# Moving the later modulation sums of a transformer layer from the matmul engine to GpSimd

## The chip, the cores and the metric

The kernel runs on one core of one Trainium2 chip. Five engines of the core work side by side, each on its own instructions in order: TensorE (PE in the profile; PEld is its weight load), VectorE (DVE), ScalarE (ACT), GpSimd (POOL) and SyncE (SP), which here only issues transfers. An engine that waits holds up everything behind it on that engine. The metric is the device time of one execution in microseconds, as a median over runs.

## The reference

One layer of a diffusion backbone on 512 latent tokens of width 1024 with 256 context tokens. All numbers are float32. What matters here is where the conditioning vector `c` enters:

```python
def adaln(cond, w_mod, b_mod):                  # cond (1, 1024), w_mod (1024, 6144)
    return jnp.split(jax.nn.silu(cond) @ w_mod + b_mod, 6, axis=-1)

sh1, sc1, g1, sh2, sc2, g2 = adaln(c, w_mod[l], b_mod[l])
hx = modulate(rmsnorm(x, norm_attn_g[l]), sh1, sc1)     # the context likewise, with c_ctx
...                                                      # projections, two kinds of attention
x = x + g1 * mixed
hx2 = modulate(rmsnorm(x, norm_ffn_g[l]), sh2, sc2)
x = x + g2 * hierarchical_moe(hx2, ...)                  # 16 experts, each token in two of them
return rmsnorm(x, final_norm_g)
```

`silu(c) @ w_mod` is a vector by a 1024 x 6144 matrix, so each weight is used once. The first 2048 columns (sh1, sc1) are needed at once; the other 4096 (g1, sh2, sc2, g2: "the later columns", 16 MB) only when the attention is done.

## The kernel before

The stages follow each other: normalise the tokens and form the first modulation (to about 60 us), project (to 120), neighbourhood attention with its projections (to 242), latent attention (to 370), output projection and routing (to 427), then the experts, whose weights stream from memory until the end. Outside of the hand-ordered parts (`manual_schedule`) a scheduler orders each engine's instructions when the kernel is built; the order is then fixed. Matmuls of float32 precision are made of three products of high and low parts (`mm3`, lines 57 to 59).

In the neighbourhood attention 32 blocks (four head pairs `p`, two heads `u`, four query tiles `i`; `b` counts them) run one after the other. A block's `na_scores` (L606, L607) go to PSUM; VectorE adds a bias and takes the row maximum (L617, L470); ScalarE takes the exponential; the next block's turn transposes it (`na_turn`, L634). Between them PE gets parts of the next pair's projections (`works`, by the table `NS`). `na_values` (L643) closes a pair.

Every second block also calls `mod_rest(n)`: two loads of 512 KB of the later columns' weights into the ring `raw` (three buffers, queue of SyncE), and four matmuls (L521) whose stationary operand is `sstat`, silu(c) in one column of 32 zeros; the four write to the four quarters of the partitions of one PSUM bank. After eight calls the sums with the bias row (`br`) go to DRAM (`mod_d`), twice in all. Later stages read `mod_d` back: g1 for the latent attention's output weights (L894), then sh2, sc2 and g2.

At the very start GpSimd issues five small loads, first `mp1` (biases and gain of the first modulation), and VectorE adds 1 to a part of it (L142) ahead of all of its normalisation work. GpSimd also fills four `ql` tiles with zeros (L532).

Of the kernel before, what the change touches and what calls it, by code (L numbers as in the profile page):

```python
# [17 lines left out]
P = 128  # L18
# [17 lines left out]
K_TRI, K_IOTA, K_TJ, K_VAL, K_ROW, K_END = 0, 128, 256, 272, 280, 281  # L36


def hybrid_kernel(tc, nc, x_k, x_q, ctx, cvec, w_mod_a, w_mod_b, b_mod_c, b_mod_r, g_ffn_row,
                  w_v, w_kv, w_ql, w_qk, g_q, g_kv, w_uq, w_ukv, rel, w_out_a, w_out_b, w_r, b_r,  # L40
                  w_gate, w_up, w_down, g_fin_row, cpk0, cpk, out):
    sy, ac, ve, pe, gp = nc.sync, nc.scalar, nc.vector, nc.tensor, nc.gpsimd
# [81 lines left out]
    mp1 = cst.tile([P, 4, 12], F32, name="mp1")  # L124
# [4 lines left out]
    ab = cst.tile([P, 4, 8], F32, name="ab")  # L129
    sm = cst.tile([P, 24], F32, name="sm")  # L130
    eps = cst.tile([P, 1], F32, name="eps")
    ve.memset(eps, EPS)
    lg = cst.tile([P, 4, 20], F32, name="lg")
# [365 lines left out]


    ya_d = tc.dram_tile([T, D], F32, name="ya_d")
    zero = nw.tile([P, 512], F32, name="zero")
    ve.memset(zero, 0.0)


    mod_d = tc.dram_tile([2, 4, 512], F32, name="mod_d")
    modf = mod_d.rearrange("r a b -> r (a b)")
    mod_ps = []

    def mod_rest(n):  # L510
        r, k = divmod(n, KT)
        if k == 0:
            br = nw.tile([P, 512], F32, name="br", tag="br", bufs=1)
            ve.memset(br, 0.0)
            rows = br.rearrange("(a b) n -> a b n", b=32)[:, 0, :]
            sy.dma_start(rows, b_mod_r[r])
            mod_ps[:] = bank(7), br, rows
        ps, br, rows = mod_ps
        ws = [load(w_mod_b[r, k, :, q * 1024:(q + 1) * 1024]) for q in range(2)]
# [200 lines left out]
    for b, (p, u, i) in enumerate(blocks):  # L720
        w = b % 8
        if w == 0 and p < 3:
            na_open(p + 1)
        s = na_scores(p, u, i)
        nm = na_max(p, u, i, s)
        if p < 3:
            if w in (3, 5, 7):
                for u_ in range(2):
                    na_part(p + 1, w // 2 - 1, u_, 1)
            if w == 2:  # L730
                na_weights(p + 1, 1, 1)
            if w == 4 and p < 2:
                na_weights(p + 2, 0, 1)
            if w == 6:
                for u_ in range(2):
                    na_bias(p + 1, u_)
        if NS[p][w] > 1:
            pull(1)
        if len(turns) >= (2 if b > 24 else 1):
            na_turn(*turns.pop(0))  # L740
        turns.append((p, u, i))
        na_exp(p, u, i, s, nm)
        if w == 0 and p:
# [541 lines left out]
    with tc.manual_schedule(engines={pe.engine, ve.engine}):  # L1285
# [55 lines left out]
        count = cst.tile([P, NE + 1 + NB * NE], I32, name="count")  # L1341
# [503 lines left out]
def _layout(**n):  # L1845
# [16 lines left out]
    a["w_mod_b"] = c(wm[:, 2048:].reshape(KT, P, 2, 2048).transpose(2, 0, 1, 3))  # L1862
# [4 lines left out]
    a["b_mod_r"] = c(bm[2048:].reshape(2, 4, 512))  # L1867
# [51 lines left out]
```

## Time and profile before

| | |
|---|---|
| median of three runs | 735.29 us (733.8 to 735.91) |
| profiled execution | 733.54 us; span 731.8 us, so 1.7 us lie around the span |
| mean granted clock of TensorE | 0.983 |
| busy: PE, DVE, ACT, POOL | 698.1, 546.4, 447.7, 83.7 us (95%, 75%, 61%, 11% of the span) |
| moved by DMA | 174.58 MB, 239 GB/s over the span |

The profile is one execution. Busy shares are means over all stages; what an edit of one stage is worth is read in that stage's rows.

### The profile page before, as it was taken

How to read it: one execution, taken by the hardware profiler on the slowest of the kernel's cores; microseconds unless marked ns; L12 is line 12 of the kernel's file. 1: busy time of each engine (PE TensorE's matmuls, PEld its weight loads, DVE VectorE, ACT ScalarE, POOL GpSimd, SP SyncE). 2: the span in 40 equal slices, each digit the busy share in tenths (PEclk: the TensorE clock that was granted, in tenths of full speed). 3: DMA queues.
4: the chain of work that ended last, by engine and by line, in shares of the span. 5: the costliest groups of instructions: out<-in, count | busy, mean ns of one | idle time of the engine just before them, and what ended most of it. 6: DMA issues, size and time to landing. Idle time of an engine off the chain costs nothing. (4 is left out here: it accounts for less than half of the span.)

```text
span 731.8 us, 10466 instructions
## 1 busy us (share of the span) xinstructions
PE 698.1 (95%) x3918; PEld 516.9 (71%) x3919; DVE 546.4 (75%) x749; ACT 447.7 (61%) x698; POOL 83.7 (11%) x56
## 2 busy tenths in 40 slices
PE   4999999999999999999999679999999999999995
PEld 3678997767765887868658557777777777777773
DVE  4572457766676795656536778999999999999996
ACT  6451355654555455646644377777777777777763
POOL 1010000000000000000010122222222222221310
PEclk9999999999999999999999769999999999999998
DMA  8931238555476821121179979999999999999673
GB/s 319 409 124 60 73 95 279 194 172 190 144 236 202 288 88 43 60 76 54 59 252 364 346 244 364 362 372 370 353 360 357 358 352 350 358 354 379 239 132 116
DMA packets 39336, 174.58 MB, mean 239 GB/s; under 512 B 5711, under 2 KB 7191, under 8 KB 26992
## 3 DMA queue, kind: packets, MB, share of 16 engines
q1 hardware_dynamic: 34880, 163.72, 61.4%
q0 software_dynamic: 4112, 10.06, 6.3%
q8 instruction: 32, 0.52, 0.3%
q14 instruction: 24, 0.20, 0.1%
q10 hardware_dynamic: 288, 0.08, 0.0%
HBM read 163.00 MB, written 14.79 MB: 243 GB/s over the span
## 5 line engine op out<-in xcount | busy, mean ns | idle before, releaser
L1376 DVE TENSOR_TENSOR el<-ew,eh 128x2048 fp32r<-128x2048 f32 (+1 forms) x106 | 220.6, 2087 | 17.3 <-ACT eh L1373 13.7
L1373 ACT CAST eh<-ew 128x1024 fp32r<-128x1024 f32 x190 | 190.1, 1050 | 43.9 <-PE s L59 29.4
L57 PE MATMUL s<-eh,xh 128*96 128x512 f32 x260 | 104.7, 403 | 1.1 <-ACT xh L62 1.1
L59 PE MATMUL s<-eh,xl 128*96 128x512 f32 x260 | 103.3, 397 | 0.0
L58 PE MATMUL s<-el,xh 128*96 128x512 f32 x260 | 102.8, 395 | 0.0
L1588 POOL DMA_INDIRECT ya_d<-yo,idx x14 | 45.5, 3251 | 140.7 <-DVE yo L1592 140.7
L59 PEld LDWEIGHTS s<-eh,xl 128*96 128x96 f32 x260 | 42.3, 163 | 19.3 <-DVE xl L63 0.7
L57 PEld LDWEIGHTS s<-eh,xh 128*96 128x96 f32 x260 | 42.4, 163 | 18.3 <-ACT xh L62 1.4
L58 PEld LDWEIGHTS s<-el,xh 128*96 128x96 f32 x260 | 42.5, 164 | 17.5 <-DVE el L1376 0.2
L57 PE MATMUL y<-eh,ghh 128*96 128x512 f32 x120 | 48.2, 401 | 0.0
L59 PE MATMUL y<-eh,ghl 128*96 128x512 f32 x120 | 47.3, 394 | 0.0
L58 PE MATMUL y<-el,ghh 128*96 128x512 f32 x120 | 47.2, 393 | 0.0
L470 DVE TENSOR_REDUCE nm<-s 128x1 f32<-128x768 f32 x32 | 30.5, 954 | 19.1 <-PE s L59 18.9
L57 PE MATMUL ps<-wh,hh 128*128 128x512 f32 (+2 forms) x128 | 43.9, 345 | 0.5 <-ACT hh L275 0.3
L59 PE MATMUL ps<-wh,hl 128*128 128x512 f32 (+2 forms) x128 | 43.5, 345 | 0.2 <-DVE hl L277 0.2
L58 PE MATMUL ps<-wl,hh 128*128 128x512 f32 (+2 forms) x128 | 43.4, 341 | 0.0
L1303 POOL MEMSET xg<- 128x1024 f32 x2 | 1.9, 954 | 322.1 <-DMA g<-mod_d 322.1
L57 PE MATMUL ps<-hh,wh 128*128 128x512 f32 (+1 forms) x96 | 36.4, 379 | 0.0
L946 ACT ACTIVATE pr<-s,nm 128x768 f32<-128x768 f32 x32 | 29.1, 908 | 9.8 <-DVE nm L470 9.6
L59 PE MATMUL ps<-hh,wl 128*128 128x512 f32 (+1 forms) x96 | 34.4, 359 | 0.0
L58 PE MATMUL ps<-hl,wh 128*128 128x512 f32 (+1 forms) x96 | 34.2, 357 | 0.0
L1261 POOL DMA_INDIRECT xg<-hx_d,idx x16 | 24.2, 1510 | 65.9 <-PE t L1519 46.7
(360 smaller groups left out, 1455.8 us busy)
## 6 DMA issues: line engine op xcount, KB each, us to landing
ew<-w_gate SPq DMA_DIRECT2D x32, 1024.0 KB, 8.6
ew<-w_up SPq DMA_DIRECT2D x32, 1024.0 KB, 8.0
ew<-w_down SPq DMA_DIRECT2D x32, 1024.0 KB, 9.4
raw<-w_mod_b SPq DMA_DIRECT2D x32, 512.0 KB, 3.8
wm<-w_mod_a SPq DMA_DIRECT2D x16, 512.0 KB, 10.8
raw<-w_qk SPq DMA_DIRECT2D x8, 512.0 KB, 3.4
raw<-w_v SPq DMA_DIRECT2D x4, 512.0 KB, 10.5
ya_d<-zero SPq DMA_DIRECT2D x8, 256.0 KB, 3.2
```

The source lines that it names most:

```text
L57: pe.matmul(ps, lh, rh, start=start, stop=False)
L58: pe.matmul(ps, lh, rl, start=False, stop=False)
L59: pe.matmul(ps, ll, rh, start=False, stop=stop)
L470: ve.tensor_reduce(out=nm, in_=s, axis=AX.X, op=OP.max, negate=True)
L946: ac.activation(pr, s, AF.Exp, bias=nm, accum_out=mla_ssum[h // 2][:, t, h % 2:h % 2 + 1])
L1261: ins = gp.indirect_dma_start(out=xg[e % NX][slice(0, CAP), :], out_offset=None, in_=hx_d, in_offset=bass.IndirectOffsetOnAxis(ap=idx[slic ...
L1303: gp.memset(x_, 0.0)
L1373: ac.copy(wh[:, cs], r[:, cs])
L1376: ve.tensor_tensor(wl[:, cs], r[:, cs], f(wh[:, cs]), op=OP.subtract)
L1588: gp.indirect_dma_start(out=ya_d, out_offset=bass.IndirectOffsetOnAxis(ap=idx[rows, 1, e:e + 1], axis=0), in_=yo[rows, :], in_offset=None, ...
```

## The change

Of the later 4096 columns, cut into eight rows of 512, six rows are summed on GpSimd. Such a row's weights come in two pieces of 1 MB (128 partitions x 4 x 512; `mod_load`, twelve pieces in all, from GpSimd's own queue, into the two halves of the pool `omp`). `mod_weigh` multiplies a piece by silu(c), which stands in `sstat` for each partition, and folds its four parts by additions; the two pieces of a row are added up in `macc`. What is left is a sum over the 128 partitions: `mod_sum` does it with four small matmuls against a column of ones (L544), adds the bias on VectorE and stores the row. The last two rows stay on the matmul engine (`mod_rest`), now all in the last pair's eight blocks, with 256 instead of 512 columns a matmul. The tiles `ab`, `mp1`, `lg` and `count` move to other pools, `zero` is halved, and with `mp1` its load moves behind the four other loads of GpSimd.

```diff
-    gp.dma_start(mp1, b_mod_c)
-    ve.tensor_scalar(mp1[:, :, 4:8], mp1[:, :, 4:8], 1.0, None, op0=OP.add)
     gp.dma_start(gq, g_q)
     gp.dma_start(gkv, g_kv)
     gp.dma_start(wr, w_r)
...
+    gp.dma_start(mp1, b_mod_c)
+    ve.tensor_scalar(mp1[:, :, 4:8], mp1[:, :, 4:8], 1.0, None, op0=OP.add)
...
+    def mod_load(n):
+        w = mod_w[n] = omp.tile([P, 4, T], F32, name=f"wb{n % 2}", tag=f"{n % 2}", bufs=1)
+        gp.dma_start(w, w_mod_b[n // 2, n % 2])
+    def mod_weigh(n):
+        r, h = divmod(n, 2)
+        w = mod_w.pop(n)
+        gp.tensor_tensor(w, w, sstat[:, 4 * h:4 * h + 4, 0:1].to_broadcast([P, 4, T]), op=OP.mult)
+        gp.tensor_tensor(w[:, 0:2, :], w[:, 0:2, :], w[:, 2:4, :], op=OP.add)
+        if h == 0:
+            acc = mod_acc[r] = nw.tile([P, 512], F32, name="macc", tag="macc", bufs=2)
+            gp.tensor_tensor(acc, w[:, 0, :], w[:, 1, :], op=OP.add)
+        else:
+            gp.tensor_tensor(w[:, 0, :], w[:, 0, :], w[:, 1, :], op=OP.add)
+            gp.tensor_tensor(mod_acc[r], mod_acc[r], w[:, 0, :], op=OP.add)
+    def mod_rows(n):
+        br = nw.tile([P, n * P], F32, name="br", tag="br", bufs=1)
+        ve.memset(br, 0.0)
+        return br, br.rearrange("(a b) n -> a b n", b=32)[:, 0, :]
+    def mod_sum(r):
+        acc = mod_acc.pop(r)
+        br, rows_ = mod_rows(1)
+        sy.dma_start(rows_, b_mod_r[r])
+        ps = bank(7)
+        for g in range(4):
+            pe.matmul(ps[g * 32:(g + 1) * 32, 0:P], ones, acc[:, g * P:(g + 1) * P], start=True, stop=True,
+                      tile_position=(0, g * 32))
+        ve.tensor_tensor(br, br, ps[:, 0:P], op=OP.add)
+        sy.dma_start(mod_d[r], rows_)
...
+        w = load(w_mod_c[k])
         for g in range(4):
-            pe.matmul(ps[g * 32:(g + 1) * 32, :], sstat[:, k, :],
-                      ws[g // 2][:, g % 2 * 512:g % 2 * 512 + 512], start=(k == 0), stop=(k == KT - 1),
-                      tile_position=(0, g * 32))
+            pe.matmul(ps[g * 32:(g + 1) * 32, 0:256], sstat[:, k, :], w[:, g * 256:g * 256 + 256], start=(k == 0),
+                      stop=(k == KT - 1), tile_position=(0, g * 32))
...
-        if i % 2:
-            mod_rest(p * 4 + u * 2 + i // 2)
+        if b % 2 == 0 and b // 2 < NP:
+            if b // 2 + 2 < NP:
+                mod_weigh(b // 2)
+                mod_load(b // 2 + 2)
+            else:
+                mod_weigh(b // 2)
+        if b % 4 == 3 and b // 4 > 1:
+            mod_sum(b // 4 - 2)
+        if p == 3:
+            mod_rest(w)
```

What the scheduler made of it is seen at three places. First GpSimd, which in the kernel before does nothing between the `ql` memsets and the latent attention's end. In the changed kernel this is what it issues for one pair of pieces (`wb_1291` and `wb_1344`), up to the first multiply of the next pair (`wb_1409` and `wb_1479`); the names in brackets are the semaphores waited for (DMASW: a load of GpSimd's queue; Pool: an instruction of GpSimd itself):

```order
L523 TENSOR_TENSOR wb_1291<-wb_1291,sstat 128x2048 [waits DMASW7_49]
L524 TENSOR_TENSOR wb_1291<-wb_1291 128x1024 [waits Pool_49]
L523 TENSOR_TENSOR wb_1344<-wb_1344,sstat 128x2048 [waits DMASW0_49]
L527 TENSOR_TENSOR macc<-wb_1291 128x512 [waits Pool_49]
L524 TENSOR_TENSOR wb_1344<-wb_1344 128x1024 [waits Pool_49]
L517 DMA wb_1409<-w_mod_b 128x2048 [waits DMASW1_49,Pool_49]
L529 TENSOR_TENSOR wb_1344<-wb_1344 128x512 [waits Pool_49]
L530 TENSOR_TENSOR macc<-macc,wb_1344 128x512 [waits Pool_49]
L517 DMA wb_1479<-w_mod_b 128x2048 [waits DMASW2_49,Pool_49]
L523 TENSOR_TENSOR wb_1409<-wb_1409,sstat 128x2048 [waits DMASW1_49]
```

The load of the next pair's first piece is issued behind five of the pair's seven instructions, and the multiply that needs it stands four places behind it.

Second PE, at the end of the neighbourhood attention: the last values (`pt`,`nav`), the last transposes (`rsb`) and the first products of the latent attention (`o`). Before:

```order
L643 MATMUL ps<-pt,nav 64x512
L521 MATMUL ps<-raw,sstat 32x512 x2
L643 MATMUL ps<-pt,nav 64x512
L643 MATMUL ps<-pt,nav 64x128 x16
L643 MATMUL ps<-pt,nav 64x512 x2
L486 MATMUL ps<-c_58,rsb 128x128 x4
L57 MATMUL o<-kvh,wkh 128x512
```

and in the changed kernel:

```order
L560 MATMUL ps<-raw,sstat 32x256 x4
L672 MATMUL ps<-c_58,pr 128x128 x4
L57 MATMUL ps<-wh,kvh 128x512
L544 MATMUL ps<-macc,one 32x128 x4
L58 MATMUL ps<-wl,kvh 128x512
L59 MATMUL ps<-wh,kvo 128x512
L681 MATMUL ps<-pt,nav 64x512 x2
L681 MATMUL ps<-pt,nav 64x128 x16
L681 MATMUL ps<-pt,nav 64x512 x2
L485 MATMUL ps<-c_58,rsb 128x128 x4
L544 MATMUL ps<-macc,one 32x128 x4
L57 MATMUL o<-kvh,wkh 128x512
```

The last two of GpSimd's six rows (L544) are summed here, the sixth directly ahead of the latent attention; the other four stand at blocks 11, 15, 19 and 23.

Third VectorE at the same place (`qnl` and `onl` are the last low parts of this stage, `kl` the first of the next). Before:

```order
L525 TENSOR_TENSOR br<-br,ps 128x512 [waits PE_49]
L63 TENSOR_TENSOR qnl<-raw,qnh 128x512 [waits DMAHW2_49,Activation_49]
L63 TENSOR_TENSOR qnl<-raw,qnh 128x512 [waits DMAHW3_49,Activation_49]
L489 TENSOR_TENSOR rsb<-ps,rsb 128x512 [waits Activation_49]
L491 TENSOR_TENSOR onl<-rsb,onh 128x512 [waits Activation_49]
```

and in the changed kernel (DMAHW: a transfer of SyncE's queue):

```order
L563 TENSOR_TENSOR br<-br,ps 128x256 [waits PE_49]
L82 COPY pt<-ps 128x512 [waits PE_49]
L63 TENSOR_TENSOR qnl<-raw,qnh 128x512 [waits DMAHW0_49,Activation_49]
L63 TENSOR_TENSOR qnl<-raw,qnh 128x512 [waits DMAHW1_49,Activation_49]
L534 MEMSET br 128x128 [waits DMAHW3_49,DVE_49]
L488 TENSOR_TENSOR rsb<-ps,rsb 128x512 [waits Activation_49]
L546 TENSOR_TENSOR br<-br,ps 128x128 [waits DMAHW6_49,DVE_49]
L490 TENSOR_TENSOR onl<-rsb,onh 128x512 [waits Activation_49]
L534 MEMSET br 128x128 [waits DMAHW7_49,DVE_49]
L546 TENSOR_TENSOR br<-br,ps 128x128 [waits DMAHW0_49,DVE_49,PE_49]
L74 TENSOR_TENSOR kl_2515<-krt,kh_2512 32x768 [waits DMAHW2_49,Activation_49]
```

There is one `br` buffer, so three rounds (store the row, clear `br`, load the next bias, add) stand in a line in VectorE's order ahead of the latent attention's `kl`.

## Rows read from the trace of the kernel before

**Rows 1.** Windows, neighbourhood attention: busy us (instructions) of PE, PEld, DVE, ACT, POOL; clock; DMA.

```profile
123.00:242.00 119.00, 118.46 (x738) 79.64 (x737) 78.83 (x144) 62.88 (x132) 0.00 (x0) 1.00 0.59 194
```

**Rows 2.** Timeline of PE around the first call of mod_rest: start, length, instruction.

```profile
124.07 0.40 PE L59 MATMUL ps<-hh,wl 128*128 128x512 f32 x1
124.40 1.06 PE L521 MATMUL ps<-raw,sstat 128*32 128x512 f32 x8
125.40 0.50 PE L57 MATMUL ps<-hh,wh 128*128 128x512 f32 x1
125.74 0.40 PE L58 MATMUL ps<-hl,wh 128*128 128x512 f32 x1
```

**Rows 3.** Timeline of PE at the stage's end, with the last half call.

```profile
236.48 1.05 PE L521 MATMUL ps<-raw,sstat 128*32 128x512 f32 x4
237.47 3.68 PE L643 MATMUL ps<-pt,nav 128*64 128x512 f32 x38
...
241.49 0.48 PE L57 MATMUL o<-kvh,wkh 128*128 128x512 f32 x1
```

**Rows 4.** Timeline of PE, sums of the first modulation with 128 columns.

```profile
41.32 0.42 PE L246 MATMUL ps<-wm,sstat 128*32 128x128 f32 x6
```

**Rows 5.** Groups of POOL by form: count, busy us, mean ns, idle before.

```profile
L1192 POOL TENSOR_SCALAR oh<-ck,pos 128x96 fp32r<-128x96 f32 x6 | 3.3, 562 | 44.9 <-DVE pos L1153 44.9
...
L1303 POOL MEMSET xg<- 128x1024 f32 x2 | 1.9, 954 | 322.1 <-DMA g<-mod_d 322.1
...
L1909 POOL MEMSET const-float32-0.0<- 128x1 f32 x1 | 0.1, 99 | 0.1
```

**Rows 6.** SP's issue that frees the first buffer; DMA issues: KB each, us to landing.

```profile
107.00 0.34 SPq L411 DMA_DIRECT2D kr_dram<-krs  x1
...
raw<-w_mod_b SPq DMA_DIRECT2D x32, 512.0 KB, 3.8
```

**Rows 7.** Timeline of the start: the loads of POOL, VectorE's first wait, PE.

```profile
1.32 0.70 POOL L141 DMA_DIRECT2D mp<-b_mod_c  x1 [0.85 <-POOLq L1909]
...
3.64 0.54 POOL L146 DMA_DIRECT2D brb<-b_r  x1
...
6.50 0.17 DVE L142 TENSOR_SCALAR mp<-mp 128x16 f32<-128x16 f32 x1 [5.29 <-DMA mp<-b_mod_c]
...
13.64 1.97 PE L225 MATMUL ps<-c,xb 128*128 128x128 f32 x8 [1.87 <-DVE nwv L94]
```

**Rows 8.** Groups of DVE with two operands in SBUF, 118 to 242 us.

```profile
L564 DVE TENSOR_TENSOR wl<-raw,wh 128x1024 fp32r<-128x1024 f32 x5 | 6.1, 1222 | 7.2 <-ACT wh L561 7.2
...
L63 DVE TENSOR_TENSOR uq<-raw,uq 128x768 fp32r<-128x768 f32 x3 | 2.8, 948 | 0.0
...
L554 DVE TENSOR_TENSOR bb<-rb,cka 128x128 f32<-128x128 f32 x10 | 2.6, 284 | 0.0
```

**Rows 9.** Timeline of routing: DVE beside POOL's compares of 128x96.

```profile
415.27 0.23 DVE L1120 TENSOR_TENSOR eq<-lg 128x80 f32<-128x80 f32 x1
415.43 0.23 DVE L1121 TENSOR_TENSOR gt<-lg 128x80 f32<-128x80 f32 x1
415.58 0.30 DVE L1123 TENSOR_TENSOR eq<-eq,ck 128x80 f32<-128x80 f32 x1
```

**Rows 10.** Windows of PE around its idle time in routing: busy, clock, DMA.

```profile
412.00:416.00 4.00, 1.07 (x15) 0.60 0.95 297
...
428.00:432.00 4.00, 4.00 (x10) 0.50 0.74 236
432.00:436.00 4.00, 4.00 (x17) 0.84 0.77 274
```

**Rows 11.** Timeline of DVE: a row's sum, the next clear of br, the stage's end.

```profile
176.98 0.68 DVE L525 TENSOR_TENSOR br<-br,ps 128x512 f32<-128x512 f32 x1
...
179.75 0.48 DVE L514 MEMSET br<- 128x512 f32 x1 [0.29 <-DMA mod_d<-br]
...
244.68 0.95 DVE L74 TENSOR_TENSOR kl<-krt,kh 32x768 fp32r<-32x768 f32 x1 [0.16 <-ACT kh L69]
```

More of the change, by code (lines that the diff above doesn't have):

```diff
@@ L36, with hybrid_kernel @@
 K_TRI, K_IOTA, K_TJ, K_VAL, K_ROW, K_END = 0, 128, 256, 272, 280, 281
-def hybrid_kernel(tc, nc, x_k, x_q, ctx, cvec, w_mod_a, w_mod_b, b_mod_c, b_mod_r, g_ffn_row,
+def hybrid_kernel(tc, nc, x_k, x_q, ctx, cvec, w_mod_a, w_mod_b, w_mod_c, b_mod_c, b_mod_r, b_mod_l, g_ffn_row,
                   w_v, w_kv, w_ql, w_qk, g_q, g_kv, w_uq, w_ukv, rel, w_out_a, w_out_b, w_r, b_r,
@@ L123, in hybrid_kernel @@
     ck = cst.tile([P, K_END], F32, name="ck")
-    mp1 = cst.tile([P, 4, 12], F32, name="mp1")
     gq = cst.tile([P, 3], F32, name="gq")
@@ L128, in hybrid_kernel @@
     brb = cst.tile([P, 20], F32, name="brb")
-    ab = cst.tile([P, 4, 8], F32, name="ab")
     sm = cst.tile([P, 24], F32, name="sm")
@@ L132, in hybrid_kernel @@
     ve.memset(eps, EPS)
-    lg = cst.tile([P, 4, 20], F32, name="lg")
     lsh = cst.tile([P, 20], F32, name="lsh")
@@ L173, in hybrid_kernel @@
     cka = htp.tile([P, K_QC], F32, name="cka")
+    ab = htp.tile([P, 4, 8], F32, name="ab")
+    mp1 = htp.tile([P, 4, 12], F32, name="mp1")
+    gp.dma_start(mp1, b_mod_c)
+    ve.tensor_scalar(mp1[:, :, 4:8], mp1[:, :, 4:8], 1.0, None, op0=OP.add)
     def raw_tile():
@@ L501, in hybrid_kernel @@
     ya_d = tc.dram_tile([T, D], F32, name="ya_d")
-    zero = nw.tile([P, 512], F32, name="zero")
+    zero = nw.tile([P, 256], F32, name="zero")
     ve.memset(zero, 0.0)
-    mod_d = tc.dram_tile([2, 4, 512], F32, name="mod_d")
-    modf = mod_d.rearrange("r a b -> r (a b)")
+    mod_d = tc.dram_tile([8, 4, P], F32, name="mod_d")
+    modf = mod_d.rearrange("(h r) a b -> h (r a b)", h=2)
+    mod_acc, mod_w = {}, {}
+    one = cst.tile([P, 1], F32, name="one")
+    ve.memset(one, 1.0)
+    ones = one.to_broadcast([P, 32])
@@ new lines, in hybrid_kernel @@
+    NP = 12
+    def mod_load(n):
[12 more added lines that the diff above has]
+            gp.tensor_tensor(mod_acc[r], mod_acc[r], w[:, 0, :], op=OP.add)
@@ L508, in hybrid_kernel, with mod_rest @@
     mod_ps = []
-    def mod_rest(n):
-        r, k = divmod(n, KT)
+    def mod_rest(k):
         if k == 0:
[L513 to L519, printed above, removed]
+            br, rows_ = mod_rows(2)
+            sy.dma_start(rows_, b_mod_l)
+            mod_ps[:] = bank(7), br, rows_
+        ps, br, rows_ = mod_ps
+        w = load(w_mod_c[k])
@@ L520, in mod_rest @@
         for g in range(4):
-            pe.matmul(ps[g * 32:(g + 1) * 32, :], sstat[:, k, :],
-                      ws[g // 2][:, g % 2 * 512:g % 2 * 512 + 512], start=(k == 0), stop=(k == KT - 1),
-                      tile_position=(0, g * 32))
+            pe.matmul(ps[g * 32:(g + 1) * 32, 0:256], sstat[:, k, :], w[:, g * 256:g * 256 + 256], start=(k == 0),
+                      stop=(k == KT - 1), tile_position=(0, g * 32))
         if k == KT - 1:
-            ve.tensor_tensor(br, br, ps, op=OP.add)
@@ L526, in mod_rest @@
-            sy.dma_start(mod_d[r], rows)
+            ve.tensor_tensor(br, br, ps[:, 0:256], op=OP.add)
+            sy.dma_start(mod_d[6:8].rearrange("r a b -> (r a b)").rearrange("(g n) -> g n", g=4), rows_)
     na_heads, na_w, na_ps = {}, {}, {}
@@ L689, in hybrid_kernel @@
     na_open(0)
+    mod_load(0)
+    mod_load(1)
     for j in range(2):
@@ L782, in hybrid_kernel @@
                 for hf in range(2):
-                    sy.dma_start(ya_d[n * P:(n + 1) * P, hf * 512:hf * 512 + 512], zero)
+                    sy.dma_start(ya_d[n * P:(n + 1) * P, hf * 512:hf * 512 + 512].rearrange("p (a b) -> p a b", a=2),
+                                 zero[:, None, :].to_broadcast([P, 2, 256]))
     for tn in turns:
@@ L1079, in hybrid_kernel @@
     wp = pool("wp", side="right")
+    lg = wp.tile([P, 4, 20], F32, name="lg")
     gs = wp.tile([P, D], F32, name="gs")
@@ L1340, in hybrid_kernel @@
             pe.matmul(pc[:, 0, 0:NE], trb[:, 1, :], mh[:, t, :], start=(t == 0), stop=(t == 3))
-        count = cst.tile([P, NE + 1 + NB * NE], I32, name="count")
+        count = vq.tile([P, NE + 1 + NB * NE], I32, name="count")
         ve.tensor_copy(count[:, 0:NE], pc[:, 0, 0:NE])
@@ L1861, in _layout @@
     a["w_mod_a"] = np.concatenate([w0.reshape(1, 4, P, 1024), wa.reshape(4, 4, P, 1024)[1:]])
-    a["w_mod_b"] = c(wm[:, 2048:].reshape(KT, P, 2, 2048).transpose(2, 0, 1, 3))
+    a["w_mod_b"] = c(wm[:, 2048:5120].reshape(2, 4, P, 6, 512).transpose(3, 0, 2, 1, 4).reshape(6, 2, P, 4, 512))
+    a["w_mod_c"] = c(wm[:, 5120:].reshape(KT, P, 1024))
     bt = np.repeat(bm[:2048].reshape(2, 4, 2, P).transpose(3, 1, 0, 2).reshape(P, 4, 4), 2, axis=2)
@@ L1866, in _layout @@
     a["b_mod_c"] = c(np.concatenate([bt, gt], 2))
-    a["b_mod_r"] = c(bm[2048:].reshape(2, 4, 512))
+    a["b_mod_r"] = c(bm[2048:5120].reshape(6, 4, P))
+    a["b_mod_l"] = c(bm[5120:].reshape(4, 256))
     a["g_ffn_row"] = c(n["norm_ffn_g"])
@@ L1895, in _layout @@
     return a
-_INS = ['x_k', 'x_q', 'ctx', 'cvec', 'w_mod_a', 'w_mod_b', 'b_mod_c', 'b_mod_r', 'g_ffn_row',
+_INS = ['x_k', 'x_q', 'ctx', 'cvec', 'w_mod_a', 'w_mod_b', 'w_mod_c', 'b_mod_c', 'b_mod_r', 'b_mod_l', 'g_ffn_row',
         'w_v', 'w_kv', 'w_ql', 'w_qk', 'g_q', 'g_kv', 'w_uq', 'w_ukv', 'rel', 'w_out_a', 'w_out_b', 'w_r', 'b_r',
```

## The prediction, made before the changed kernel ran

> **What bounds the kernel now.** I read the windows by stage first, then the timeline of PE inside the stage that the change edits, then the groups of GpSimd and VectorE, last the start. In the neighbourhood attention PE is busy 118.46 of 119.00 us at full clock, VectorE 78.83, GpSimd not at all, DMA at 0.59 [rows 1]: what PE is spared there shortens the kernel, what makes PE wait lengthens it, us for us. The stages behind it follow in line, so a shift passes to the end. The sum is made against the profiled execution's own 733.54 us; the median of the runs is 1.75 us above it, and that is added at the end.
>
> **What PE is spared.** A whole call of mod_rest holds PE 1.00 us from its start to the next instruction, 0.10 ahead of it and 0.11 behind it, where the next product takes 0.34 us and not 0.23 (the 0.40 us products overlap) [rows 2]. A half call of four records costs as much, 0.99 us [rows 3]: 1.2 us either way. The stage has 13 whole calls (first at 124.40) and six halves (last at 236.48), 19 x 1.2 = 22.8 us. One more wait of 0.5 us for their loads goes too. In their place come eight calls with half the columns, half of 1.0 plus 0.2, so 0.7 us each or 5.6; and six sums of 128 columns at 0.42 [rows 4] plus 0.15, 3.4 in all. Spared: 23.3 - 9.0 = **14.3 us**. PE, unhindered, would reach the latent attention, now at 241.49 [rows 3], at 227.2.
>
> **When GpSimd is done.** That is the term that decides, since the sixth sum stands in PE's order directly ahead of that point. Per pair GpSimd issues two multiplies of 2048 elements, two additions of 1024 and three of 512; 46,080 elements in 42 instructions in all. The trace has no GpSimd instruction with two inputs. A memset of 1024 takes 0.954 us, one of a single element 0.099 [rows 5]: 0.83 ns an element for one pass. That is the lower bound, reads and write at once. The upper one is the compare of 128x96, 0.562 us, or 4.8 ns an element if the start is 0.1 us as well [rows 5]. Two inputs and an output are two or three passes, 1.7 to 2.5 ns; I take 2.1, near the memset row, since the compare is so short that its time may be mostly a start. Then 2048 elements take 4.4 us, 1024 take 2.25, 512 take 1.2.
>
> The first piece can be loaded when kr_dram is stored: issued at 107.00 [rows 6] and 2.1 us under way, as the store of a row was from 177.66 to 179.75 [rows 11]. 512 KB land in 3.8 us on SyncE's queue [rows 6]; GpSimd's first small load took 5.2 from issue to use, 1.32 to 6.50 [rows 7]. For 1 MB on that queue I take 6.5. So: multiply from 115.6, next load issued at 120.0, its multiply from 126.5, the pair folded and the third piece asked for at 134.4, there at 140.9. From then a pair takes 14.5 us to the issue of the next load, then 6.5 to its landing, under which lie only two additions and another issue (0.7, rows 7): 21.0 us a pair. Five pairs from 140.9, the last of 16.9: 241.8; each instruction waits for the one before it, 0.1 us for some 30 of them: **245**. At 1.7 ns the pair takes 18.1 and the end is 227, no wait; at 0.83 ns about 190; at 4.8 ns about 350. The Trainium skill (GPSIMD Engine Reference, section 3.1) gives 4497 ns for a GpSimd tensor_tensor of 2048 float32, measured elsewhere; by it, estimated in proportion for the shorter ones, the end would come within a few us of that, and no run so far shows the instruction.
>
> So PE waits 245 - 227.2 = 17.8 us in all for the sums, some 4 of them already at block 23, the rest at the last row: +17.8 against -14.3, **+3.5**. Behind PE in this wait stand the latent attention's products, on SyncE's queue the expert loads and g1; nothing else is there to fill it.
>
> **What else moves.** (a) mp1's load is now fifth on GpSimd: issued at about 3.6 instead of 1.32, it lands 2.3 to 3 us later, and VectorE, which waited for it until 6.50, holds all its normalisation behind it [rows 7]. The second lot of transposes, at 13.64, waits for VectorE; some of the delay was a wait for x anyway, so I take **+2.0** (0 to 2.8). It shifts GpSimd's start as well. (b) PE idle for over 10 us loses its clock: in routing it fell to 0.60 within 412 to 416 and came back in 432 to 436, some 5 us after steady work had begun [rows 10]; half of 5 us is **+2.5** (0 to 4). (c) VectorE has three rounds through the one `br` buffer: four transfers of 2.1 us and the additions, 9.4 us, from the last call of mod_rest, which stands about 2 us ahead of where it was at 236.48; in the old scale it ends at about 244.5, and `kl` began at 244.68 [rows 11]. Hidden by the wait for GpSimd; without that cover it has no margin, and 1 MB of w_out ahead of the small loads may add 1.4. (d) At block 12 the clear of `br` waits for a store that stands behind a bias load: about 2.5 us of VectorE, mostly in its own idle time (119.00 - 78.83, rows 1); 0.5 on PE without the cover. (e) Loads: the same bytes, at a DMA share of 0.59; 1 KB rows of the zero fill instead of 2 KB, hidden. (f) The `ql` memsets move from 44 to about 110 us, 12 us ahead of their first use: nothing.
>
> Sum: 733.5 + 3.5 + 2.0 + 2.5 = 741.5, and 1.75 to the median: **743**. Its own range is 738 to 752 (price of an element 1.95 to 2.5 ns, clock and start at their bounds).
>
> **The rivals.**
> GpSimd keeps pace (the faster side). If an element costs under 1.7 ns, or the loads land in 4 us, the end is at or before 227 and PE never waits. Then -14.3 + 2.0 + 0.5 + 1.4 = -10.4, or **725** as a median (721 to 731). For it: the memset row is far below. Against it: two inputs. It decides from a period of 18 us a pair.
>
> The wait eats the gain exactly: GpSimd ends between 235 and 239, the time is 733 to 737.
>
> VectorE and GpSimd take turns at the memory. In this stage VectorE has 35 instructions with both operands in SBUF, 20 us in all; the three largest groups are 11.5 us of them [rows 8]. If each must stand alone with a GpSimd instruction, GpSimd loses up to those 20 us (end at 262 to 265) and VectorE waits half of a GpSimd instruction, time-weighted 1.6 us, some 30 times: 48 us beside its 40 us of idle time. PE waits until about 260: -14.3 + 33 + 2.0 + 2.5 = +23, **758** (752 to 764). In the trace the only such neighbours are the compares at 415: VectorE's instructions start 0.16 us apart beside GpSimd's of 0.55, which speaks against whole instructions in turn, but those read only 96 elements [rows 5, 9]. The Trainium skill (SBUF — State Buffer, Who interferes with whom) says just this, that a VectorE instruction with two SBUF inputs and a GpSimd one that reads SBUF exclude each other for the whole instruction. By that rule it is this case; rows 9 do not bear it out at their size, and nothing larger is there.
>
> GpSimd is far slower, towards the compare's price: over 764.
>
> **How the numbers follow.** Forecast 0.32, turns 0.21, far slower 0.06, exact 0.14, keeps pace 0.27. Faster by over 0.3% (2.2 us, about what a measurement of this kernel can tell) is the pace case, 0.27; the same 0.14; slower the rest, 0.59. The range reaches from the middle of the pace case to the turns case, 724 to 760, and leaves out about 0.1 at either end.
>
> **What would show it.** Right: the mean of the 128x2048 multiply on GpSimd 4 to 5 us and about 21 us from pair to pair; L544 the largest wait of PE, for POOL, over 10 us; the latent attention's first product later than 241.5; mp's addition on VectorE at 8.8 to 9.5. The turns case: L564 and L63 on VectorE far above 1.22 and 0.95 us, or started late with GpSimd busy, and GpSimd's gaps filled by them. The pace case: no wait of PE for POOL. I am wrong if the period of a pair is under 19 us, or if PE waits mostly for VectorE instead of GpSimd.

## The result and the profile after

The changed kernel takes **763.07 us** (762.44 to 763.47, four runs) against 734.54 us for the kernel before beside it: ratio 1.039, 95% interval 1.037 to 1.042, slower. The prediction was 743 us with a range of 724 to 760. Some kernels below have a few executions more than 1.5% longer than their fastest; ratios and intervals leave these out, the medians do not.

The head of the page of the changed kernel; the busy times of PE and ScalarE are as before, VectorE is 40 us busier (546.4 before), GpSimd 107 us (83.7 before):

```profile
span 761.3 us, 10488 instructions
...
PE 697.8 (92%) x3902; PEld 522.8 (69%) x3903; DVE 586.6 (77%) x760; ACT 447.4 (59%) x698; POOL 190.7 (25%) x110
```

Where the 29.5 us of span came in is read from three starts on PE. The first product of L57 stood at 20.67 us before and stands at 24.54 now (+3.9). The latent attention's first product, 241.49 in [rows 3], stands here (timeline of PE, changed kernel):

```profile
256.22 0.64 PE L560 MATMUL ps<-raw,sstat 128*32 128x256 f32 x8 [0.25 <-DMA raw<-w_mod_c]
260.41 0.64 PE L560 MATMUL ps<-raw,sstat 128*32 128x256 f32 x8
261.80 0.42 PE L544 MATMUL ps<-macc,one 128*32 128x128 f32 x8
...
269.26 0.50 PE L57 MATMUL o<-kvh,wkh 128*128 128x512 f32 x1
```

That is +27.8, so 24 us were lost between the two, and some 2 us more behind the second. The store of `kr_dram`, at 107.00 in [rows 6], is issued at 110.86, still 3.9 us late: the 24 us belong to the neighbourhood attention. Windows of that stage, which [rows 1] showed as one row with PE full and a clock of 1.00:

```profile
123.00:150.00 27.00, 20.01 (x95) 16.77 (x96) 19.41 (x25) 9.75 (x19) 19.56 (x11) 0.81 0.65 220
150.00:180.00 30.00, 24.63 (x137) 18.46 (x136) 28.98 (x30) 10.75 (x23) 25.64 (x12) 0.89 0.33 114
180.00:210.00 30.00, 28.71 (x183) 21.24 (x182) 26.41 (x42) 15.90 (x33) 25.89 (x15) 1.00 0.42 146
210.00:240.00 30.00, 23.35 (x142) 17.03 (x142) 27.86 (x33) 13.05 (x28) 28.52 (x13) 0.83 0.39 132
```

PE is idle for 20 of these 117 us and slow in part of the rest; VectorE, the third pair of numbers, is 88 to 97% busy from 150 on. Why is read from its groups by shape (busy us, mean ns), 118 to 262 us:

```profile
L469 DVE TENSOR_REDUCE nm<-ps 128x1 f32<-128x512 f32 x32 | 21.9, 686 | 0.5
L592 DVE TENSOR_TENSOR bb<-rb,cka 128x128 f32<-128x128 f32 x14 | 21.7, 1574 | 0.0
L589 DVE TENSOR_TENSOR bb<-rb,cka 128x256 f32<-128x256 f32 x7 | 14.9, 2125 | 2.5 <-DMA rb<-rel 2.5
...
L602 DVE TENSOR_TENSOR wl<-raw,wh 128x1024 fp32r<-128x1024 f32 x5 | 10.1, 2018 | 4.3 <-ACT wh L599 4.3
...
L628 DVE SCALAR_TENSOR_TENSOR ql<-ps,qh 64x512 fp32r<-64x512 f32 x8 | 5.5, 685 | 1.4 <-ACT qh L626 1.4
```

The bias additions `bb`, 284 ns in [rows 8], take 1574 (1412 over all 16, with two that run before 118 us); `wl` takes 2018 instead of 1222. Both have two operands in SBUF, the memory of the tiles. The maxima `nm` (one operand, from PSUM) and `ql` (one of two from PSUM) take what they took in the kernel before (118 to 242 us):

```profile
L470 DVE TENSOR_REDUCE nm<-ps 128x1 f32<-128x512 f32 x32 | 22.0, 689 | 0.7
...
L590 DVE SCALAR_TENSOR_TENSOR ql<-ps,qh 64x512 fp32r<-64x512 f32 x6 | 4.1, 688 | 0.7 <-ACT qh L588 0.6
```

GpSimd's two largest groups; its timeline at the end of the first pair of pieces, at its two longest waits behind that, and at the end of the last pair; then waits of PE:

```profile
L523 POOL TENSOR_TENSOR wb<-wb,sstat 128x2048 f32<-128x2048 f32 x12 | 43.4, 3615 | 14.0 <-DMA wb<-w_mod_b 13.9
L524 POOL TENSOR_TENSOR wb<-wb 128x1024 f32<-128x1024 f32 x12 | 31.1, 2590 | 0.5
```

```profile
139.48 1.30 POOL L530 TENSOR_TENSOR macc<-macc,wb 128x512 f32<-128x512 f32 x1
...
147.31 3.61 POOL L523 TENSOR_TENSOR wb<-wb,sstat 128x2048 f32<-128x2048 f32 x1 [5.65 <-DMA wb<-w_mod_b]
...
182.12 1.31 POOL L527 TENSOR_TENSOR macc<-wb 128x512 f32<-128x512 f32 x1 [5.92 <-PE ps L544]
...
245.00 1.29 POOL L530 TENSOR_TENSOR macc<-macc,wb 128x512 f32<-128x512 f32 x1
```

```profile
PE ps L672 <- ACT pr L662: 13.1, 9, 3.2
PE ps L57 <- DVE ql L628: 8.1, 1, 8.1
PE ps L544 <- DVE br L546: 1.8, 1, 1.8
```

PE has no wait for GpSimd in this stage. It waits for `ql`, and for exponentials that stand behind VectorE's maxima (ScalarE waited 42.1 us for `nm`, 11.7 before). The timeline of all engines shows how the 8.1 us arose:

```profile
121.31 3.60 POOL L523 TENSOR_TENSOR wb<-wb,sstat 128x2048 f32<-128x2048 f32 x1 [5.30 <-DMA wb<-w_mod_b]
121.55 3.65 DVE L589 TENSOR_TENSOR bb<-rb,cka 128x256 f32<-128x256 f32 x1 [2.46 <-DMA rb<-rel]
124.92 0.57 POOL L517 DMA_DIRECT2D wb<-w_mod_b  x1
125.12 3.10 DVE L592 TENSOR_TENSOR bb<-rb,cka 128x128 f32<-128x128 f32 x2
125.51 2.35 POOL L524 TENSOR_TENSOR wb<-wb 128x1024 f32<-128x1024 f32 x1
...
128.40 0.69 DVE L628 SCALAR_TENSOR_TENSOR ql<-ps,qh 64x512 fp32r<-64x512 f32 x1
...
129.24 0.55 PE L57 MATMUL ps<-hh,wh 128*128 128x256 f32 x1 [8.07 <-DVE ql L628]
```

An addition of 0.41 us starts 0.24 us behind GpSimd's multiply and ends at 125.20, 0.29 us behind that one's end; the next two end 0.36 us behind GpSimd's addition. A wait for the memory is thus counted as busy time: it stands in no list of waits, only in a mean that is too long. `ql` is queued behind, and PE behind `ql`. About 2.5 of the 8.1 us are another thing: the bias row `rel` landed late (2.46, the second line), which no addition waited for in the kernel before.

### The profile page after: what moved, and what is told of

Its sections match the earlier page's. It is cut to its first block, busy times and chain, and to the rows that moved or that the text cites. A ratio compares the mean times of both kernels' runs of the same rounds, so it can differ in the third digit from the quotient of the medians.

```text
span 761.3 us, 10488 instructions
## 1 busy us (share of the span) xinstructions
PE 697.8 (92%) x3902; PEld 522.8 (69%) x3903; DVE 586.6 (77%) x760; ACT 447.4 (59%) x698; POOL 190.7 (25%) x110
## 4 chain that ended last, share of the span: by engine, by line
PE 61%; DVE 13%; DMA 6%; ACT 2%; issue 2%; SPq 0%; DVEq 0%; ACTq 0%
PE s L57 10%; PE s L59 10%; PE s L58 10%; PE y L57 4%; PE y L59 4%; PE y L58 4%; PE o L1017 3%; PE tr L1008 3%; DVE bb L592 2%; DVE bb L589 2%; PE t L1569 1%; DVE nm L469 1%; DMA ew<-w_gate 1%; DVE wl L602 1%; DMA hx_d<-t 1%
## 5 line engine op out<-in xcount | busy, mean ns | idle before, releaser
L57 PE MATMUL s<-eh,xh 128*96 128x512 f32 x260 | 103.9, 400 | 0.9 <-ACT xh L62 0.9
L59 PEld LDWEIGHTS s<-eh,xl 128*96 128x96 f32 x260 | 42.1, 162 | 18.7 <-DVE xl L63 0.6
L57 PEld LDWEIGHTS s<-eh,xh 128*96 128x96 f32 x260 | 42.3, 163 | 17.9 <-ACT xh L62 1.2
L57 PE MATMUL y<-eh,ghh 128*96 128x512 f32 x120 | 48.1, 401 | 0.0
L523 POOL TENSOR_TENSOR wb<-wb,sstat 128x2048 f32<-128x2048 f32 x12 | 43.4, 3615 | 14.0 <-DMA wb<-w_mod_b 13.9
L662 ACT ACTIVATE pr<-ps,nm 128x512 f32<-128x512 f32 x32 | 22.0, 686 | 42.3 <-DVE nm L469 42.1
L57 PE MATMUL ps<-hh,wh 128*128 128x512 f32 (+1 forms) x96 | 38.7, 403 | 8.1 <-DVE ql L628 8.1
L57 PE MATMUL ps<-wh,hh 128*128 128x512 f32 (+2 forms) x128 | 43.9, 345 | 0.4 <-ACT hh L274 0.3
L58 PE MATMUL ps<-wl,hh 128*128 128x512 f32 (+2 forms) x128 | 43.3, 341 | 0.0
L59 PE MATMUL ps<-hh,wl 128*128 128x512 f32 (+1 forms) x96 | 37.0, 385 | 0.0
```

What stands on the lines that cost most here:

```text
L57: pe.matmul(ps, lh, rh, start=start, stop=False)
L58: pe.matmul(ps, lh, rl, start=False, stop=False)
L59: pe.matmul(ps, ll, rh, start=False, stop=stop)
L523: gp.tensor_tensor(w, w, sstat[:, 4 * h:4 * h + 4, 0:1].to_broadcast([P, 4, T]), op=OP.mult)
L662: ac.activation(pr, s, AF.Exp, bias=nm, accum_out=na_ssum[p][:, i, u:u + 1])
```

## The experiments

Theory: VectorE's instructions with two operands in SBUF and GpSimd's reads of SBUF exclude each other. Rivals: GpSimd's loads, its place in PE's order, the start, the rounds at the stage's end. Ratios are to the kernel before on the same chip; it took 734.1 to 735.0 us in each group of runs.

**The start.** mp1's load is issued first again:

```diff
-    gp.dma_start(gq, g_q)
-    gp.dma_start(gkv, g_kv)
-    gp.dma_start(wr, w_r)
-    gp.dma_start(brb, b_r.to_broadcast([P, 20]))
...
     gp.dma_start(mp1, b_mod_c)
+    gp.dma_start(gq, g_q)
+    gp.dma_start(gkv, g_kv)
+    gp.dma_start(wr, w_r)
+    gp.dma_start(brb, b_r.to_broadcast([P, 20]))
```

> The changed kernel with mp1's load issued first on GpSimd again, ahead of the four other small loads. Theory (the start is a term of its own, 3.8 to 3.9 us at the first product of L57, and passes to the end): first product of L57 back at about 20.7 us, time 763.1 - 3.9 = 759 us. Rival (the later stages wait for something that the start does not move, the GpSimd loads or the turns at the memory): the product moves, the end by less than 1.5 us, 762 us or more.

759.43 us (1.0345, 1.0318 to 1.0373): 3.6 us less. The term is its own and passes to the end.

**GpSimd writes, but reads nothing.**

```diff
-        gp.tensor_tensor(w, w, sstat[...].to_broadcast([P, 4, T]), op=OP.mult)
+        for _ in range(2):
+            gp.memset(w, 0.0)
...
```

> The changed kernel, GpSimd's multiplies and additions replaced by memsets of about the same busy time on the same tiles, behind the same loads: GpSimd writes, but reads nothing (the six rows then hold the biases alone). Theory (VectorE's instructions with two operands in SBUF wait for GpSimd's reads): the 128x128 bias additions back from 1412 to about 285 ns, the 128x256 ones from 1911 to about 410, the 128x1024 differences from 1719 to about 1225; the time 734.5 - 14.3 + 3.9 and 2 to 6 for the chain of br rounds, 726 to 730 us. Rival (GpSimd's mere activity, its loads or its place in PE's order cost the time): VectorE's durations stay above 1 us, time 755 us or more.

743.54 us (1.0108, 1.0075 to 1.0140), 19.5 us under the changed kernel. VectorE's groups and PE's largest wait:

```profile
L606 DVE TENSOR_TENSOR wl<-raw,wh 128x1024 fp32r<-128x1024 f32 x5 | 6.1, 1221 | 3.7 <-ACT wh L603 3.7
...
L596 DVE TENSOR_TENSOR bb<-rb,cka 128x128 f32<-128x128 f32 x12 | 3.1, 281 | 0.0
```

```profile
PE ps L564 <- DMA raw<-w_mod_c: 5.6, 1, 5.6
```

VectorE's durations are within 3 ns of those before the change: the theory holds for them. The time is 14 to 18 us above what I expected. PE waited 5.6 us of that for a load of mod_rest that was late beside two of GpSimd's pieces (issued at 215.78 and 217.67); the rest is not in these lines.

**The contention alone**, put into the kernel before: GpSimd multiplies and adds on two cleared tiles that nothing reads, in rounds of the change's sizes. In the second run each instruction reads one operand; in the third it reads none.

```diff
+        if b % 2 == 0 and b // 2 < 12:
+            dummy(b // 2)     # tensor_tensor | tensor_scalar(w, w, 1.0) | memset
```

> The kernel before, unchanged in its sums, with twelve rounds of GpSimd multiplies and additions of the changed kernel's sizes on two cleared tiles that nothing uses, no loads for them, some 85 us in a row from about 118 us. Theory (turns at the memory): VectorE's two-operand instructions of that stretch are as long as in the changed kernel (128x128 near 1.4 us), and PE, which here has no spare time, waits for them: 748 to 765 us. Rival (the loss of the changed kernel is in its loads, its sums or its order): VectorE as in the kernel before, 733 to 737 us.

> The kernel before with GpSimd's idle rounds as in the run of 758.3 us, but each instruction reads one operand (a multiplication by a constant) in place of two. Theory (any read of SBUF by GpSimd holds the path that VectorE's second operand needs): the 128x128 additions of VectorE above 0.8 us while GpSimd runs, the time some 0.4 to 1 of the 24 us longer, by how long GpSimd is at work, 743 to 758 us. Rival (only GpSimd's instructions with two operands get in the way): 734 us, the additions at 284 ns.

> The kernel before with the same idle rounds made of memsets of about the same busy time: GpSimd works as long, but reads nothing. Theory: 733 to 736 us and the 128x128 additions at 284 ns. Rival (a busy GpSimd costs VectorE or the shared memory something as such): 740 us or more.

758.33 us (1.0319, 1.0281 to 1.0357), 755.38 (1.0186, 1.0126 to 1.0247), 738.26 (1.0059, 1.0036 to 1.0083). By the ratios the reads cost 19 us with two operands and 9 with one, against the memsets, with PE's own work unchanged. With one operand, only durations are taken from the profile (an execution of 761.80 us): VectorE's `bb` and `wl`, and GpSimd's largest:

```profile
L575 DVE TENSOR_TENSOR wl<-raw,wh 128x1024 fp32r<-128x1024 f32 x6 | 18.7, 3120 | 4.5 <-ACT wh L572 3.7 <-ACT qst L421 0.8
...
L565 DVE TENSOR_TENSOR bb<-rb,cka 128x128 f32<-128x128 f32 x16 | 11.1, 726 | 0.0
```

```profile
L533 POOL TENSOR_SCALAR wb<-wb 128x2048 f32<-128x2048 f32 x12 | 64.3, 5366 | 0.2
```

The memsets should have cost nothing and cost 3.9 us. There is another contention at 107 us, in all three runs, beside the memsets that clear the two tiles and `ql` (VectorE's four took 1.41 us before):

```profile
107.30 1.81 POOL L705 MEMSET wb<- 128x2048 f32 x1 [103.13 <-DMA kr_dram<-krs]
107.38 3.97 DVE L416 TENSOR_SCALAR qlt<-qlt,sm 128x384 f32<-128x384 f32 x4
```

PE waits 1.7 us for these `qlt`; where the rest of the 3.9 us comes from is not settled.

**Shorter instructions.** First each GpSimd instruction in pieces of 256 elements, then the pieces chained so that each waits for the end of the one ahead.

```diff
-        gp.tensor_tensor(w, w, sstat[...].to_broadcast([P, 4, T]), op=OP.mult)
+        for a in range(4):
+            for o in range(0, T, 256):
+                v = w[:, a, o:o + 256]
+                gp.tensor_tensor(v, v, sstat[...].to_broadcast([P, 256]), op=OP.mult)
...
+            tc.add_manual_dep(ins.ins, pieces[-1], ...)     # second run only
```

> The changed kernel with each GpSimd instruction cut into pieces of 256 elements a partition: the same reads, shorter instructions (0.45 to 0.65 us by the rates seen). Theory (an instruction holds the read path until it ends, and the other engine gets it then): VectorE's 128x128 additions fall from 1412 to some 500 to 700 ns, its lengthening in all from 40 to some 10 to 15 us, and the time to 735 to 745 us. Rival (the two engines share a rate, or GpSimd's next piece goes ahead of a waiting VectorE): VectorE's durations stay as they are, time 760 us or more, GpSimd's end no earlier.

> The changed kernel with the pieces of 256 elements again, but every GpSimd piece waits for the end of the piece ahead of it, so that GpSimd pauses between any two. Theory (a waiting VectorE instruction gets the read path only where GpSimd pauses; in the pieces that stood back to back a 128x512 difference waited 4.1 us through eight of them): the 128x128 additions at 0.3 to 0.9 us, VectorE's lengthening 5 to 15 us in all, the time 740 to 750 us, of which 3.9 are the start. Rival (the size or the pause does not matter, the two share a rate): VectorE as with the pieces back to back, 765 us or more.

769.25 us (1.0476, 1.0435 to 1.0516) and 780.17 (1.0627, 1.0577 to 1.0676): worse, both. With the pieces unchained:

```profile
212.88 4.68 DVE L63 TENSOR_TENSOR wl<-raw,wh 128x512 fp32r<-128x512 f32 x1
212.98 0.62 POOL L527 TENSOR_TENSOR wb<-wb,sstat 128x256 f32<-128x256 f32 x1
...
216.98 1.17 POOL L530 TENSOR_TENSOR wb<-wb 128x256 f32<-128x256 f32 x1
```

A difference of 0.68 us waits through eight independent multiplies and gets in at the first addition, which has to wait for them. So short instructions in a row can hold the path like a long one. They did not always: the 128x128 additions fall from 1574 to 875 ns, while those of 128x512 rise from 2382 to 2945, and VectorE is busy 581.0 us in all, 6 less than in the changed kernel. Why the time is longer all the same is not settled; one wait of PE is 6.5 us for a late load of mod_rest. Chained, VectorE is nearly free, as expected, but GpSimd is too slow: a piece of 256 elements takes 650 to 850 ns, as unchained, where an eighth of the 2048 multiply is 452, and there is a pause behind each. PE waits for it:

```profile
L607 DVE TENSOR_TENSOR bb<-rb,cka 128x128 f32<-128x128 f32 x14 | 5.9, 442 | 0.0
```

```profile
PE ps L559 <- POOL macc L526: 37.3, 6, 8.9
```

**The stage's end, and what is left without turns.** mod_rest in the first pair's blocks, with mp1 first: alone, with chained pieces, with GpSimd writing only, and with that and next to no load traffic.

```diff
-        if p == 3:
+        if p == 0:
             mod_rest(w)
...
-        gp.dma_start(w, w_mod_b[n // 2, n % 2])
+        gp.dma_start(w[:, :, 0:8], w_mod_b[n // 2, n % 2, :, :, 0:8])     # last run only
```

> The changed kernel with mp1's load first and the eight calls of mod_rest in the first pair's blocks instead of the last pair's, so that the fifth and sixth sum no longer wait for their bank; GpSimd as in the changed kernel. Theory (three rounds through br and the loads of the last calls stood bare at the end of the stage): 759.4 less 3 to 7, 752 to 756 us, the last sums not behind the last values in a row. Rival (these are covered by VectorE's lateness): 758 to 761 us.

> Both: the pieces of 256 that wait for each other, mp1's load first, mod_rest in the first pair's blocks. Theory (what is left of the turns is 5 to 12 us of PE): 734.5 - 14.3 and 5 to 12, that is 725 to 733 us, faster than the kernel before. Rival (GpSimd with 190 instructions is now too late, the last sums wait for POOL): 738 us or more, with L559 waiting for POOL.

> GpSimd's arithmetic replaced by memsets as before (the six rows hold the biases alone), with mp1's load first and mod_rest in the first pair's blocks: no turns, no late start, no rounds at the end. Theory (PE is spared 14.3 us and the rest of the loss is those three): 734.5 - 14.3 and 0 to 2, 720 to 723 us. Rival (the spared time of PE was put too high): 728 us or more.

> The run with mp1's load first, mod_rest early and GpSimd writing only (735.2 us, PE idle 8.1 us in 100 to 242 us, of it 5.6 behind a late load of w_uq and of rel), but of each 1 MB piece only 8 of 512 columns are loaded; the memsets stay, and the rows hold the biases alone. Theory (what is left of the loss is the traffic of GpSimd's loads beside SyncE's): 720 to 725 us, no wait of PE behind ScalarE's casts. Rival (PE has less spare work to lose than 14.3 us, the blocks' own chain over VectorE and ScalarE bounds them): 731 us or more, idle time of PE as before.

759.55 us (1.0359), 783.58 (1.0677), 735.16 (1.0004, 0.9978 to 1.0031) and 724.63 (0.9868, 0.9830 to 0.9906). The end of the stage gave nothing while VectorE was late anyway. With chained pieces PE again waited for POOL (43.3 us). Without reads the time is that of the kernel before, not the 720 that I expected; without GpSimd's traffic too, a gain is there, though the six rows then hold no sums. From 100 to 242 us PE idles some 8 us with the traffic and 0.7 without. What the traffic did, by the rows of the third run: the bias rows `rel` and a `w_uq` tile landed late, and PE or ScalarE, with the exponentials behind it, stood.

```profile
117.84 0.42 DVE L593 TENSOR_TENSOR bb<-rb,cka 128x256 f32<-128x256 f32 x1 [2.27 <-DMA rb<-rel]
...
119.34 0.35 PE L57 MATMUL ps<-hh,wh 128*128 128x256 f32 x1 [1.97 <-DVE ql L632]
...
219.81 0.83 ACT L62 CAST uq<-raw 128x768 fp32r<-128x768 f32 x1 [2.58 <-DMA raw<-w_uq]
```

The last run takes the traffic away; it does not move it back to SyncE's queue. The kernel before had the same bytes there and PE idle for 0.5 us [rows 1], so it is not the bytes alone; whether it is the queue, the size of the pieces or their time was not tried. The latent attention's first product in that run:

```profile
230.49 0.50 PE L57 MATMUL o<-kvh,wkh 128*128 128x512 f32 x1
```

**The fourth corner:** the turns without the traffic (sums of what stands in the tiles).

> The run with mp1's load first and mod_rest early (759.6 us), GpSimd's multiplies and additions kept, but of the pieces behind the first two only 8 of 512 columns are loaded (the rows then hold sums of what stood in the tiles). If the two losses add up, the load traffic's 10.5 us come off: 748 to 750 us, 24 us above the run of 724.6 us that has neither. If they cover each other (PE late for one reason no longer waits for the other), 755 to 760 us.

771.86 us (1.0462, 1.0369 to 1.0554): neither. It is not faster without the loads but, if anything, slower (1.0359 with them). One stretch of the timeline:

```profile
225.85 12.32 DVE L596 TENSOR_TENSOR bb<-rb,cka 128x128 f32<-128x128 f32 x1
226.26 7.18 POOL L527 TENSOR_TENSOR wb<-wb,sstat 128x2048 f32<-128x2048 f32 x2
233.40 4.62 POOL L528 TENSOR_TENSOR wb<-wb 128x1024 f32<-128x1024 f32 x2
238.10 1.80 POOL L533 TENSOR_TENSOR wb<-wb 128x512 f32<-128x512 f32 x1
```

An addition of 0.28 us takes 12.32, until two multiplies and two additions on different tiles are done (238.02). The one of 512 elements waits for the one ahead, and VectorE gets in. The 128x128 additions mean 3964 ns here, 1508 in the run with the loads. By the ratios the turns cost some 44 us here (1.0462 - 0.9868 of 734.4) instead of 24. That GpSimd's waits for loads had been VectorE's openings is my reading, not shown: all in all GpSimd waited no less here (12.4 us for loads, 18.7 for sums on PE) than with the loads (20.8 and 5.5).

**Fewer conflicting instructions:** the bias additions on GpSimd itself.

```diff
-        ve.tensor_tensor(bb[:, 0, :], rb, cka[...], op=OP.add)
+        gp.tensor_tensor(bb[:, 0, :], rb, cka[...], op=OP.add)
...
```

> The run with mp1's load first and mod_rest early (759.6 us), with the bias additions (24 instructions a stage, whose lengthening is some 28 of VectorE's 40 us) issued by GpSimd instead of VectorE, in GpSimd's own order between its multiplies. Theory (the turns cost by way of VectorE's two-operand instructions, and those left are the five 128x1024 differences and some of 512 and 768 elements): VectorE's busy time in 123 to 240 us near 90 instead of 110 us, the time down by half to three quarters of the 24 us, 741 to 748 us. Rival (GpSimd, with 12 us more to do, is the bound and the sums or the bias come too late): 755 us or more, PE or VectorE waiting for POOL.

756.15 us (1.0305, 1.0271 to 1.0339): 3.4 us less, which the two intervals do not tell apart. The time lies in the rival's range, but not for its reason: PE waits for POOL 3.1 us in all, VectorE not at all. The theory's premise was off: VectorE is busy 85.2 us from 123 to 240, but 91.9 and not 110 in the run that it is compared with. GpSimd is denser, and the instructions left on VectorE wait longer (128x768 takes 950 ns without contention, and 2080 in the run compared with):

```profile
L63 DVE TENSOR_TENSOR uq<-raw,uq 128x768 fp32r<-128x768 f32 x3 | 10.3, 3420 | 0.0
L490 DVE TENSOR_TENSOR onl<-rsb,onh 128x512 fp32r<-128x512 f32 x3 | 9.9, 3315 | 0.1
```

**Without GpSimd.** In the kernel before, VectorE multiplies and adds up half of each call's tiles, a quarter, then whole calls (the first eight; four of each eight; three of each eight).

```diff
+            ve.scalar_tensor_tensor(acc, ws[q], sstat[:, k, 0:1], acc, op0=OP.mult, op1=OP.add)
...
-        for g in range(4):
+        for g in range(2):      # half of each call; whole calls leave out all four
```

> The kernel before, in which VectorE instead of GpSimd takes half of the later columns: of each call of mod_rest it multiplies one of the two loaded tiles (128x1024) by silu(c) and adds it up, and PE sums over the partitions at the end of each row pair with two matmuls against ones. No GpSimd, no other queue, the loads as before. PE is spared two of four matmuls in 16 calls, about 0.5 us each, less 1.5 for the sums: 6 to 7 us. VectorE gets 16 instructions of 1.2 us, 19.5 us beside its 40 us of idle time. Theory (PE's spared time is real where neither turns nor loads of another queue take it back): 727 to 730 us. Rival (the blocks' chain over VectorE has no room for instructions of 1.2 us, as it had none for the lengthened ones): 734 us or more, PE waiting for ScalarE's exponentials behind VectorE.

> The same for the first eight calls of mod_rest alone (a quarter of the later columns): PE is spared 3 to 3.5 us, VectorE gets 9.8 us. Theory: 731 to 732 us. Rival (each added VectorE instruction delays a block): 734 us or more.

> The kernel before, in which VectorE takes eight whole calls of mod_rest (both tiles of each of the first eight, the first 2048 of the later columns) and PE sums the result over the partitions with four matmuls. The two runs before this spared PE nothing, since the matmuls for the four quarters of the partitions run side by side: two of them took 1.04 us, as four had. Whole calls spare it 7 x 1.2 = 8.4 us; VectorE gets 19 us, all in the first half of the stage. Theory (spared time of PE counts where no engine takes turns with VectorE and no other queue loads): 726 to 729 us. Rival (the blocks have no room on VectorE): 735 us or more, PE waiting behind VectorE.

> The same amount spread out: of each eight calls VectorE takes the second, fourth, fifth and sixth, PE the others and one sum more. PE is spared 2 x 3 x 1.2 = 7.2 us, VectorE gets 19 us over the whole stage. Theory: 727 to 730 us. Rival: 735 us or more.

> The same with the third to fifth call of each eight: PE is spared 2 x 2 x 1.2 = 4.8 us, VectorE gets 14 us. Theory: 730 to 731 us. Rival: 735 us or more.

738.74, 738.84, 737.12, 735.03 (1.0016, 0.9997 to 1.0035) and 737.17 us: none faster. The first two could not spare PE anything, which [rows 3] had said already: a matmul of one quarter is two records, and one quarter takes what four take (eight records, 1.06 us in [rows 2]):

```profile
178.31 1.04 PE L536 MATMUL ps<-raw,sstat 128*32 128x512 f32 x2
179.29 0.50 PE L57 MATMUL ps<-hh,wh 128*128 128x512 f32 x1
```

In the others PE has short waits that the kernel before lacks (5.7 us from 100 to 243 us in the fourth, 0.5 before), and the scheduler splits some calls in two, at full price each. How much either takes of the 5 to 8 us spared is not settled. No version here that computes the sums beats the kernel before.

## Why the prediction was wrong

The step that failed is the choice of what PE would wait for: "PE waits 245 - 227.2 = 17.8 us in all for the sums", that is for GpSimd. It waits for VectorE. The mechanism stood among the rivals as the turns at the memory, at 758 us and 0.21, and was put behind because the compares of [rows 9] showed none of it. Those rows do show none, at 80 to 96 elements; why not there is open, and beside GpSimd's instructions of 512 to 2048 elements it shows. The sign that I had named for being wrong came: PE waits for VectorE itself (9.9 us for `ql` and `br`) and by way of ScalarE (13.1 us), not for GpSimd. The rule of the Trainium skill (SBUF — State Buffer, Who interferes with whom), that a VectorE instruction with two SBUF inputs contends with a GpSimd one that reads SBUF, but not with one that only writes, is what the runs show: 1574 ns beside reads, 281 beside memsets.

The account of the 28.7 us, along one path of runs: work that PE is spared -9.8 (from 734.4 to 724.6, without reads and traffic), GpSimd's traffic +10.5 (to 735.2), reads instead of writes +24.4 (to 759.6), mod_rest's place 0, the start +3.6. The fourth corner shows that another order of the steps would share it out differently, and by the intervals each step is known to 2 to 4 us.

- **PE spared 14.3**: right in sign, too high. Without reads and traffic the latent attention begins at 230.49, 11.0 us earlier than in [rows 3]; where the other 3 us are is not settled.
- **GpSimd done at 245**: its last instruction ends at 246.3, and from the first pair's `macc` (139.48) to the last (245.00) a pair takes 21.1 us, as predicted, but by errors that cancel. The multiply takes 3.6 us, not 4.4; the first starts at 121.3, not 115.6, of which 3.9 are the start of the kernel. Two pairs take 24 to 25 us, with a wait of 5.65 us for a load in one and of 5.92 us for PE's sum, which frees `macc`, in the other; three take 18.4 to 19.4. GpSimd's additions took some 7 us in all more than at their shortest. The last two sums did not wait for GpSimd: they stood behind mod_rest's last call (260.41), whose bank VectorE had read at 261.53.
- **(a) the start, +2.0**: 3.6 to 3.9; mp1 is used at 10.67 instead of 6.50 [rows 7], 4.2 us later and not 2.3 to 3.
- **(b) the clock, +2.5**: too small, since PE idled again and again, not once. (1 - clock) x busy in the windows above, an estimate, is 3.8 + 2.7 + 4.0 = 10.5 us, in the three windows where PE waited most; no single wait there is longer than 8.1 us.
- **(c) the rounds through `br`, hidden**: yes, but by VectorE's lateness. Without GpSimd's reads they show, with the late load: 743.5 against 735.2 with mod_rest early, of which 3.6 are the start.
- **(e) the loads, nothing**: wrong by 10.5 us where no turns cover it. The bytes are the same, but with 1 MB pieces on a second queue small, urgent loads of the first landed late.
- **The turns' price, 758**: near 763, but by luck. I had GpSimd lose 20 us and PE wait for it; GpSimd lost little and VectorE most.

## What to carry to other kernels

Before work goes to GpSimd, list VectorE's instructions with two operands in SBUF on the path beside it. In these traces each could wait until GpSimd next waited for something, and not just until its instruction ended. The profile shows this as a longer mean of one shape, not as a wait, so compare means by shape first. And that the sum of the bytes stays the same does not make it free to move them to another queue in larger pieces: here that cost some 10 us.

## What was not expected of the hardware

- Independent GpSimd instructions in a row can keep a waiting VectorE instruction out: 0.28 us became 12.32 beside four of them.
- GpSimd reads with one operand exclude it too (128x128 additions of 726 ns), and a tensor_scalar of 2048 elements (5.37 us) is slower than the multiply with two operands (3.6 us).
- A VectorE tensor_scalar from SBUF to SBUF stretches beside a GpSimd memset: four of 128x384 took 3.97 us for 1.41.
- Matmuls for the four quarters of the partitions run side by side: one takes 1.04 us, four 1.06.
